# The first layer's projections on x times the norm weights, with the reciprocal root applied behind the products

## The chip, the cores and the metric

The kernel runs on one NeuronCore of a Trainium2 chip. The metric is device time in microseconds of one execution on that core, the lowest being best. Engines are named as the profile names them: PE multiplies matrices, DVE works on vectors, ACT computes activations and copies, POOL is the general engine, SP issues most of the DMAs. Each engine works through its own list of instructions.

## The reference, cut to what matters

A two-layer encoder over 256 tokens of width 1024. Each layer starts with a root mean square norm and one wide projection, whose output is cut into eleven parts.

```python
def rms_norm(x, g):
    y = xf * lax.rsqrt(jnp.mean(xf * xf, axis=-1, keepdims=True) + EPS)
    return (y * g).astype(x.dtype)

u = rms_norm(h, g_mix_pre)
(gq, gk, gv, gg, ra_f, ra_b, aq, ak, av, gate_a, gate_b) = jnp.split(u @ w_in, offsets, axis=-1)
```

`ra` gives the decay of a gated linear attention branch with `gq`, `gk`, `gv` and the output gate `gg`; `aq`, `ak`, `av` feed a grouped attention branch, in which q and k are normed once more per head and turned by rotary tables; the two gates mix the branches. Then follow an output projection, a gated feed-forward part and a per-layer embedding, each with its own norms. All data are float32; the products must have about that accuracy.

## The kernel before

**Products.** A product in float32 accuracy is made of three passes over operands split in a high part (fp32r) and a low remainder: high x high, high x low, low x high. Weights come from HBM in units of about 1 MB into two `raw` buffers. ACT casts a unit to its high part `wh` in two pieces, DVE subtracts to get the low part `wl` (`split`, line 130), and a `raw` buffer is loaded again when DVE has read it. Four `wh`/`wl` pairs exist, so casts run ahead of PE by a few units. The class `Stream` (line 245) gives out loads and splits in the order of the plan. Activations are kept transposed and split the same way in `uT`, a tile for each four of the eight 128-column blocks k of the 1024 columns, with the two token halves (hf) side by side.

**Stages.** In layer 0 the order is: the start (x, its norm, the first weights), the `rq` stage with the ranks and the attention's q (four weight units of 256 rows by 1056 columns, six accumulators: two token halves by the three column pieces of `RQ`), `kv`, `gqk`, `v`, `gg`, the gates, and so on. Layer 1 has the same stages with its norm made in another place.

**What sets the order.** The instruction order within an engine is partly written out: `on` (line 139) puts each instruction behind the one that the same engine got from `on` before it. All else is placed by a scheduler, which works from the order of the program, priorities and the dependences. Small tasks that have to wait for something are generators: each `tick` of a projection step lets them come nearer to their next part (`yield n` means after n ticks). `start` (line 792) is such a task.

**The start before.** x of the first token half is loaded in two parts by two queues, then the first weight unit in two pieces with x of the second half between them. Per half, ACT squares the first 512 columns (`square`), DVE the rest (`square_here`), POOL makes the reciprocal root (`rstd`), DVE multiplies x by it (`normed`, line 758), PE transposes the result, and ACT and DVE make high and low parts with the norm weight as a per-partition factor (`turned`, line 773), since behind the transpose the columns lie on partitions. The norm weights come as eight rows and are transposed by PE (`gains`, line 763). Before that PE multiplies constants (`warm_up`). `rq_first` (line 967) orders the first unit's products so that they start with what is there first.

**Behind the products.** `put_q` (line 945) squares the attention's q per head on ACT (`head_ss`), POOL makes the roots (`inv_sqrt`, line 447 and behind), DVE turns q with the rotary tables (`rope`). `put_ranks` (line 918) splits the 32 rank columns on DVE. `keys` (line 1003) does the same for k and splits v of the attention. The q and k of the linear branch are made transposed, with columns on partitions and tokens along the row, and are copied out of PSUM by ACT. The linear branch's v is split, its gate copied, and the mixing gates go through a sigmoid on ACT.

Of the kernel before, what the change touches and what calls it, by code (L numbers as in the profile page):

```python
# [10 lines left out]
F32 = mybir.dt.float32  # L11
# [39 lines left out]
WARM = 7, 3, 1  # L51
# [7 lines left out]
def trunk_kernel(ctx: ExitStack, tc: tile.TileContext, a: dict, out: bass.AP):  # L59
# [83 lines left out]

    keep = cp.tile([P, 512], BF16, tag="keep", name="keep")
# [5 lines left out]
    def load_x(hf, queues=(("dma", nc.sync), ("dma", nc.sync))):  # L150
        for j, (e, q) in enumerate(queues):
            c = slice(j * 512, (j + 1) * 512)
            on(e, q.dma_start, h[:, hf, c], a["x"][0, hf * P : (hf + 1) * P, c])

    load_x(0, (("dma", nc.sync), ("act", nc.scalar)))
# [612 lines left out]

    def split_here(hi, lo, src):
        on("act", nc.scalar.copy, hi, src)  # L770
        on("dve", nc.vector.tensor_tensor, out=lo, in0=src, in1=hi.bitcast(F32), op=ALU.subtract)

    def turned(hf, k, n):

        ps = aux()
        for i in range(n):
            on("pe", nc.tensor.transpose, ps[:, i * P : (i + 1) * P], xn[hf][:, (k + i) * P : (k + i + 1) * P], ident)
        hi, lo = uT.at(k, n, hf * P, P)
        if n == 4:
            y = t512()  # L780
# [11 lines left out]
    def start():  # L792
# [34 lines left out]
        for hf in range(2):  # L827
            normed(hf, 4, 4)
# [754 lines left out]
```

## Time and profile before

| what | value |
|---|---|
| device time, median of 3 runs | 924.73 us (923.97 to 925.41) |
| span of the profiled execution | 922.9 us |
| median of the runs less that span | 1.8 us |
| PE busy | 912.2 us, 99% of the span |
| DVE busy | 786.1 us, 85% |
| ACT busy | 578.5 us, 63% |
| POOL busy | 83.8 us, 9% |
| mean DMA rate | 188 GB/s |
| mean granted TensorE clock | 0.998 |

The profile is of one execution of its own, so its span is set beside the timed runs and not equal to them. A row of the order of time gives the start in us, the time from there to the end, the engine, the line of the kernel, the operation, what it writes and reads, and how many were put together; in brackets stands how long the engine was idle just before and what ended that. A name that ends in q (SPq, ACTq) is a queue that issues DMAs. A line 142 is the helper `on`, and the rows there are told apart by their tiles: `h` is x, `big_start` a tile of `uT`, `raw`, `wh` and `wl` the weights. Matmuls overlap, so their pace is read from one row's start to the next.

### The profile page before, as it was taken

To read this page: it belongs to the slowest core of one execution; us is meant where nothing else is said; L and a number is where in the kernel's file an instruction comes from. 1 tells how busy PE (TensorE), PEld (TensorE's weight loads), DVE (VectorE), ACT (ScalarE), POOL (GpSimd) and SP (SyncE) were. 2 spreads that over 40 slices of the span, in tenths; PEclk is the share of its full clock that TensorE was granted. 3 is DMA by queue.
4 is the path that set the end of the run, shared out by engine and by line. 5 is a ranking of instruction groups with operands and counts; after the bars stand their busy time and mean duration, and the time that the engine had idled before them with its cause. 6 is when DMAs were issued, how large, how long until landed. Compare 5 with 4: busy or idle time off the path is not lost.

```text
span 922.9 us, 12406 instructions
## 1 busy us (share of the span) xinstructions
PE 912.2 (99%) x4668; PEld 776.2 (84%) x4668; DVE 786.1 (85%) x1002; ACT 578.5 (63%) x954; POOL 83.8 (9%) x147
## 2 busy tenths in 40 slices
PE   9999999999999999999999999999999999999996
PEld 6898888888888888888899988888888888888885
DVE  6898989987579998999779789798875799989884
ACT  4669676664567656566676677765644766565563
POOL 3400211300000000000114001100001000000000
PEclk9999999999999999999999999999999999999999
DMA  7463455656286565647576424454573756545361
GB/s 260 144 230 134 148 173 188 201 193 232 90 277 222 178 233 168 265 128 268 188 256 220 153 92 137 137 191 174 195 260 104 268 177 204 223 177 217 126 239 45
DMA packets 88679, 173.44 MB, mean 188 GB/s; under 512 B 3422, under 2 KB 26470, under 8 KB 88108
## 3 DMA queue, kind: packets, MB, share of 16 engines
q1 hardware_dynamic: 88460, 172.40, 54.0%
q8 instruction: 36, 0.59, 0.3%
q10 hardware_dynamic: 160, 0.27, 0.1%
q14 instruction: 23, 0.19, 0.1%
HBM read 169.50 MB, written 3.15 MB: 187 GB/s over the span
## 4 chain that ended last, share of the span: by engine, by line
PE 94%; DVE 2%; ACT 1%; DMA 1%; issue 1%; POOL 0%; POOLq 0%; DVEq 0%; ACTq 0%; SPq 0%
PE acc_0ffnin L120 12%; PE acc_1ffnin L120 11%; PE acc_1gate L120 7%; PE acc_0gate L120 7%; PE acc_0ffnin L104 7%; PE acc_1ffnin L104 7%; PE acc_1rq L120 3%; PE acc_0gqk L120 2%; PE acc_0wout L120 2%; PE acc_1gqk L120 2%; PE acc_1ple L120 2%; PE acc_0ple L120 2%; PE acc_0gg L120 2%; PE acc_1gg L120 2%; PE acc_0v L120 2%; PE acc_1merge L120 2%
## 5 line engine op out<-in xcount | busy, mean ns | idle before, releaser
L104 PE MATMUL acc_0ffnin<-wh_0ffnin,big_0ffnin 128*128 128x512 f32 x176 | 56.9, 393 | 0.0
L104 PE MATMUL acc_1ffnin<-wh_1ffnin,big_1ffnin 128*128 128x512 f32 x176 | 56.8, 392 | 0.0
L132 ACT CAST wh_1ffnin<-raw_1ffnin 128x1024 fp32r<-128x1024 f32 x38 | 38.5, 1049 | 27.3 <-DMA raw_1ffnin<-in_w_ffn_out_dram 8.7
L132 ACT CAST wh_0ffnin<-raw_0ffnin 128x1024 fp32r<-128x1024 f32 x38 | 38.4, 1048 | 23.8 <-PE acc_0ffnin L120 7.8
L128 DVE TENSOR_TENSOR wl_1ffnin<-raw_1ffnin,wh_1ffnin 128x1024 fp32r<-128x1024 f32 x38 | 45.0, 1221 | 8.9 <-ACT wh_1ffnin L132 8.9
L128 DVE TENSOR_TENSOR wl_0ffnin<-raw_0ffnin,wh_0ffnin 128x1024 fp32r<-128x1024 f32 x38 | 44.8, 1220 | 7.1 <-ACT wh_0ffnin L132 7.0
L120 PE MATMUL acc_1ffnin<-wh_1ffnin,big_1wout 128*128 128x512 f32 x168 | 42.5, 393 | 0.0
L120 PE MATMUL acc_0ffnin<-wh_0ffnin,big_0wout 128*128 128x512 f32 x168 | 42.5, 393 | 0.0
L104 PEld LDWEIGHTS acc_0ffnin<-wh_0ffnin,big_0ffnin 128*128 128x128 f32 x176 | 33.0, 188 | 7.1 <-DVE big_0ffnin L128 0.5
L104 PEld LDWEIGHTS acc_1ffnin<-wh_1ffnin,big_1ffnin 128*128 128x128 f32 x176 | 33.1, 188 | 6.7
L128 DVE TENSOR_TENSOR wl_1ffnin<-lent_1ffnin,wh_1ffnin 128x1024 fp32r<-128x1024 f32 x30 | 35.8, 1218 | 1.7 <-ACT wh_1ffnin L132 1.7
L128 DVE TENSOR_TENSOR wl_0ffnin<-lent_0ffnin,wh_0ffnin 128x1024 fp32r<-128x1024 f32 x30 | 35.8, 1216 | 1.7 <-ACT wh_0ffnin L132 1.7
L120 PEld LDWEIGHTS acc_1ffnin<-wh_1ffnin,big_1wout 128*128 128x128 f32 x168 | 31.1, 188 | 6.2
L120 PEld LDWEIGHTS acc_0ffnin<-wh_0ffnin,big_0wout 128*128 128x128 f32 x168 | 31.1, 188 | 6.2
L132 ACT CAST wh_1ffnin<-lent_1ffnin 128x1024 fp32r<-128x1024 f32 x30 | 30.7, 1053 | 7.1 <-PE acc_1ffnin L104 3.9
L132 ACT CAST wh_0ffnin<-lent_0ffnin 128x1024 fp32r<-128x1024 f32 x30 | 30.7, 1054 | 6.7 <-PE acc_0ffnin L104 3.9
L104 PE MATMUL acc_0ffnin<-wl_0ffnin,big_0ffnin 128*128 128x512 f32 x88 | 34.3, 389 | 0.0
L104 PE MATMUL acc_1ffnin<-wl_1ffnin,big_1ffnin 128*128 128x512 f32 x88 | 34.3, 389 | 0.0
L128 DVE TENSOR_TENSOR wl_1gate<-raw_1gate,wh_1gate 128x1024 fp32r<-128x1024 f32 x20 | 23.6, 1219 | 5.4 <-ACT wh_1gate L132 5.3
L128 DVE TENSOR_TENSOR wl_0gate<-raw_0gate,wh_0gate 128x1024 fp32r<-128x1024 f32 x20 | 23.7, 1226 | 4.8 <-ACT wh_0gate L132 4.8
L132 ACT CAST wh_0gate<-raw_0gate 128x1024 fp32r<-128x1024 f32 x20 | 20.0, 1048 | 11.7 <-DMA raw_0gate<-in_w_o_attn_dram 5.6
L132 ACT CAST wh_1gate<-raw_1gate 128x1024 fp32r<-128x1024 f32 x20 | 20.0, 1049 | 11.5 <-DMA raw_1gate<-in_w_o_attn_dram 5.5
(695 smaller groups left out, 2691.8 us busy)
## 6 DMA issues: line engine op xcount, KB each, us to landing
raw_0ffnin<-in_w_ffn_out_dram SPq DMA_DIRECT2D x11, 1024.0 KB, 6.6
raw_1ffnin<-in_w_ffn_out_dram SPq DMA_DIRECT2D x11, 1024.0 KB, 5.1
lent_0ffnin<-in_w_ffn_in_dram SPq DMA_DIRECT2D x6, 1024.0 KB, 7.4
lent_1ffnin<-in_w_ffn_in_dram SPq DMA_DIRECT2D x6, 1024.0 KB, 8.3
raw_0v<-in_w_in_dram SPq DMA_DIRECT2D x4, 1024.0 KB, 4.9
raw_0gate<-in_w_o_gla_dram SPq DMA_DIRECT2D x4, 1024.0 KB, 4.9
raw_0gate<-in_w_o_attn_dram SPq DMA_DIRECT2D x4, 1024.0 KB, 5.1
raw_0wout<-in_w_ffn_in_dram SPq DMA_DIRECT2D x8, 512.0 KB, 4.9
```

The lines of the kernel that those rows point to most:

```text
L104: return nc.tensor.matmul(o, lhsT, rhs, start=start, stop=stop)
L120: nc.tensor.matmul(o, x, y, start=start and n == 0, stop=stop and n == len(seq) - 1, **kw)
L128: nc.vector.tensor_tensor(out=out, in0=in0, in1=in1, op=ALU.subtract)
L132: nc.scalar.copy(hi, src)
```

## The change

The first layer's projections read x times the norm weights. The reciprocal root, one number for each token, is left out of the products and applied behind them, at every place where a result leaves PSUM:

- q and k of the attention: the squares are taken of the product times the root (a `scale` of the activation), and the root of the head norm is multiplied by the token's root on POOL, one operation more (`inv_sqrt` with `by`).
- ranks, v of the attention, v of the linear branch: the cast and the subtraction take the root as a per-partition factor (`split_by` and in `put_ranks`).
- the gate `gg` and the two sigmoids: a `scale` of the activation.
- q and k of the linear branch have tokens along the row. For them the 256 roots are spread over all partitions: two diagonal matrices on DVE, two matmuls with ones on PE, a copy on ACT into `spread`; the copies out of PSUM become multiplications by it on DVE.

The start is laid anew. PE transposes x itself (`turn`), ACT makes the high part (`high`), DVE the low part (`rest`), block by block; squares and roots follow after the second unit's splits, and the rotary tables' loads and products move behind them. The loads go in the order x columns 0 to 511 of the first half, first weight unit in two pieces, second unit, x columns 512 to 1023 of both halves, all by SP; the norm weights and then x columns 0 to 511 of the second half by ACT. ACT casts the first weight piece in three parts. The products of the first unit go block by block over both halves. The warm-up is six matmuls of 128 columns on a constant from POOL, six of 512, and two of 128 behind the first transposes.

```diff
-WARM = 7, 3, 1
+WARM = 6, 6, 2
...
+    seed = cp.tile([P, P], BF16, tag="seed", name="seed")
+    on("pool", nc.gpsimd.memset, seed, 1.0)
...
-    def load_x(hf, queues=(("dma", nc.sync), ("dma", nc.sync))):
-        for j, (e, q) in enumerate(queues):
-            c = slice(j * 512, (j + 1) * 512)
-            on(e, q.dma_start, h[:, hf, c], a["x"][0, hf * P : (hf + 1) * P, c])
-    load_x(0, (("dma", nc.sync), ("act", nc.scalar)))
+    def load_x(hf, j, e="dma", q=nc.sync):
+        c = slice(j * 512, (j + 1) * 512)
+        on(e, q.dma_start, h[:, hf, c], a["x"][0, hf * P : (hf + 1) * P, c])
+    load_x(0, 0)
+    on("act", nc.scalar.dma_start, grow, a["g_mix_pre"][0].rearrange("(k p) -> k p", p=P))
+    load_x(1, 0, "act", nc.scalar)
...
-    def inv_sqrt(t, n, mul, add):
+    def inv_sqrt(t, n, mul, add, by=None):
...
+        if by is not None:
+            with in_turn():
+                last_pow[0] = nc.gpsimd.tensor_scalar(out=t, in0=t, scalar1=by, scalar2=None, op0=ALU.mult)
+    def split_by(hi, lo, src, r):
+        if r is None:
+            return split(hi, lo, src)
+        nc.scalar.activation(hi, src, AF.Copy, bias=0.0, scale=r)
+        nc.vector.scalar_tensor_tensor(
+            out=lo, in0=src, scalar=r, in1=hi.bitcast(F32), op0=ALU.mult, op1=ALU.subtract
+        )
...
-    x1 = [lambda: load_x(1)]
-    on("act", nc.scalar.dma_start, grow, a["g_mix_pre"][0].rearrange("(k p) -> k p", p=P))
-    ws.load(lambda: x1 and x1.pop()())
...
+    ws.load()
+    load_x(0, 1)
+    load_x(1, 1)
...
-    def warm_up(n):
+    def warm_up(n, wide=False):
+        x = keep if wide else seed
         for _ in range(n):
-            on("pe", mm, warm, keep[:, 0:P], keep, True, True)
+            on("pe", mm, warm[:, 0 : x.shape[-1]], seed, x, True, True)
...
+    warm_up(WARM[1], True)
...
-    ss, rs, xn = [small(2, "ss") for _ in range(2)], [small(1, "rstd") for _ in range(2)], [mid(), mid()]
+    ss = [small(2, "ss") for _ in range(2)]
+    rs, spread, ropes_first = [small(1, "rs", 2) for _ in range(2)], [], []
...
-    def normed(hf, k, n):
-        c = slice(k * P, (k + n) * P)
-        on("dve", nc.vector.tensor_scalar, out=xn[hf][:, c], in0=h[:, hf, c], scalar1=rs[hf], scalar2=None, op0=ALU.mult)
...
+    def low(hi, lo, src):
+        on("dve", nc.vector.tensor_tensor, out=lo, in0=src, in1=hi.bitcast(F32), op=ALU.subtract)
...
-        on("dve", nc.vector.tensor_tensor, out=lo, in0=src, in1=hi.bitcast(F32), op=ALU.subtract)
-    def turned(hf, k, n):
...
+        low(hi, lo, src)
+    banks = {}
+    def turn(hf, *ks):
+        if (hf, ks[0] // 4) not in banks:
+            banks[hf, ks[0] // 4] = aux()
+        for k in ks:
+            ps = banks[hf, k // 4][:, k % 4 * P : (k % 4 + 1) * P]
+            on("pe", nc.tensor.transpose, ps, h[:, hf, k * P : (k + 1) * P], ident)
+    def high(hf, *ks):
+        for k in ks:
+            ps = banks[hf, k // 4][:, k % 4 * P : (k % 4 + 1) * P]
+            on("act", nc.scalar.activation, uT.at(k, 1, hf * P, P)[0][:, 0, :], ps, AF.Copy, bias=0.0, scale=gcol[:, k : k + 1])
+    def rest(hf, *ks):
+        for k in ks:
+            ps = banks[hf, k // 4][:, k % 4 * P : (k % 4 + 1) * P]
+            hi, lo = (t[:, 0, :] for t in uT.at(k, 1, hf * P, P))
+            on("dve", nc.vector.scalar_tensor_tensor, out=lo, in0=ps, scalar=gcol[:, k : k + 1],
+               in1=hi.bitcast(F32), op0=ALU.mult, op1=ALU.subtract)
...
...
-        square(0, 0)
-        square_here(0, 1)
...
-        warm_up(WARM[1])
-        rstd(0)
-        on("act", nc.scalar.copy, unit_a[0], unit_a[2])
-        normed(0, 0, 2)
-        low(*first)
-        turned(0, 0, 2)
+        turn(0, 0)
+        turn(1, 0)
+        turn(0, 1)
+        turn(1, 1)
+        turn(0, 2, 3)
...
-        square(1, 0)
-        square_here(1, 1)
-        rstd(1)
-        low(*rest)
-        normed(1, 0, 2)
-        split_here(*unit_b)
+        high(0, 0)
+        high(1, 0)
+        for c in RQ:
+            on("act", nc.scalar.copy, *(t[:, slice(*c)] for t in unit_a[::2]))
+        rest(0, 0)
+        rest(1, 0)
+        low(*cut(unit_a, slice(0, 288)))
+        high(0, 1)
+        high(1, 1)
+        low(*cut(unit_a, slice(288, 1056)))
+        on("act", nc.scalar.copy, unit_b[0], unit_b[2])
+        rest(0, 1)
+        rest(1, 1)
+        high(0, 2, 3)
+        low(*unit_b)
+        rest(0, 2, 3)
...
-        turned(1, 0, 2)
-        normed(0, 2, 2)
-        normed(1, 2, 2)
-        yield 3
+        turn(1, 2, 3)
+        high(1, 2, 3)
+        rest(1, 2, 3)
+        yield 4
...
-        turned(0, 2, 2)
...
-        turned(1, 2, 2)
...
         for hf in range(2):
-            normed(hf, 4, 4)
+            square(hf, 0)
...
+        turn(0, 4, 5, 6, 7)
+        for hf in range(2):
+            square_here(hf, 1)
+            rstd(hf)
+        ropes_first.extend(rope_tables(0))
+        high(0, 4, 5, 6, 7)
+        rest(0, 4, 5, 6, 7)
+        yield 1
+        turn(1, 4, 5, 6, 7)
+        high(1, 4, 5, 6, 7)
+        rest(1, 4, 5, 6, 7)
...
+        both = mid()
+        diag, ones = both[:, 0:T], both[:, T : T + P]
+        nc.gpsimd.memset(ones, 1.0)
         for hf in range(2):
-            turned(hf, 4, 4)
+            s = slice(hf * P, (hf + 1) * P)
+            nc.vector.tensor_scalar(out=diag[:, s], in0=ident, scalar1=rs[hf], scalar2=None, op0=ALU.mult)
+        yield 4
+        ps = aux()
+        for hf in range(2):
+            s = slice(hf * P, (hf + 1) * P)
+            mm(ps[:, s], ones, diag[:, s], True, True)
+        spread.append(both[:, 512 : 512 + T])
+        nc.scalar.copy(spread[0], ps[:, 0:T])
...
+        rows = [None, None] if l else rs
...
+            ropes = ropes_first
...
-                ropes = rope_tables(0)
-            wup = up_weights(0)
+                wup = up_weights(0)
...
-        def head_ss(src, n, junk, ss):
+        def head_ss(src, n, junk, ss, hf):
+            by = {} if rows[hf] is None else {"scale": rows[hf]}
...
-                nc.scalar.activation(junk[:, s], src[:, s], AF.Square, accum_out=ss[:, i : i + 1])
+                nc.scalar.activation(junk[:, s], src[:, s], AF.Square, accum_out=ss[:, i : i + 1], **by)
...
...
+                else:
+                    nc.vector.tensor_scalar(
+                        out=r[:, :, 0:16].bitcast(F32R), in0=src, scalar1=rows[hf], scalar2=None, op0=ALU.mult
+                    )
+                    nc.vector.scalar_tensor_tensor(
+                        out=r[:, :, 32:48].bitcast(F32R), in0=src, scalar=rows[hf], in1=r[:, :, 0:16],
+                        op0=ALU.mult, op1=ALU.subtract,
+                    )
...
-                head_ss(src, n, dst, ss[:, hd : hd + n])
-                inv_sqrt(ss[:, hd : hd + n], n, 1.0, P * EPS)
+                head_ss(src, n, dst, ss[:, hd : hd + n], hf)
+                inv_sqrt(ss[:, hd : hd + n], n, 1.0, P * EPS, rows[hf])
...
-        def rq_first(os_, hf):
...
+        def rq_first(os_):
+            for k in range(2):
+                for hf, ps in ((0, (0, 2)), (1, (0, 2)), (0, (1,)), (1, (1,))):
...
-                            mm(os_[b][:, : c1 - c0], x, y, k + p == 0, False)
-                tick()
+                            mm(os_[hf, b][:, : c1 - c0], x, y, k + p == 0, False)
+                    tick()
...
-            elif b == 2:
-                rq_first([o[hf, i] for i in range(3)], hf)
+            elif (hf, b) == (1, 2):
+                rq_first(o)
...
-                    head_ss(o[hf], 2, kr, ss)
-                    inv_sqrt(ss, 2, 1.0 / P, EPS)
+                    head_ss(o[hf], 2, kr, ss, hf)
+                    inv_sqrt(ss, 2, 1.0 / P, EPS, rows[hf])
...
-                    split(avh[:, s], avl[:, s], o[hf][:, 256:512])
+                    split_by(avh[:, s], avl[:, s], o[hf][:, 256:512], rows[hf])
...
-                if x == 0:
+                if l == 0:
+                    nc.vector.scalar_tensor_tensor(
+                        out=dst, in0=src, scalar=1.0 if x else P**-0.5,
+                        in1=spread[0].unsqueeze(1).broadcast_to([P, 2, T]), op0=ALU.mult, op1=ALU.mult,
+                    )
+                elif x == 0:
...
         for j in range(2):
             for hf, o in enumerate(project(uT)):
-                split(*(t[:, hf, j * 512 : (j + 1) * 512] for t in v), o)
+                split_by(*(t[:, hf, j * 512 : (j + 1) * 512] for t in v), o, rows[hf])
...
             for hf in range(2):
-                nc.scalar.copy(gg[:, hf, j * 512 : (j + 1) * 512], o[hf])
+                dst = gg[:, hf, j * 512 : (j + 1) * 512]
+                if rows[hf] is None:
+                    nc.scalar.copy(dst, o[hf])
+                else:
+                    nc.scalar.activation(dst, o[hf], AF.Copy, bias=0.0, scale=rows[hf])
...
-                nc.scalar.activation(sgate[br][:, hf, j * 512 : (j + 1) * 512], src, AF.Sigmoid)
+                by = {} if rows[hf] is None else {"scale": rows[hf]}
+                nc.scalar.activation(sgate[br][:, hf, j * 512 : (j + 1) * 512], src, AF.Sigmoid, **by)
```

More of the change, by code (lines that the diff above doesn't have):

```diff
@@ L792, in start @@
+    def rest(hf, *ks):
[4 more added lines that the diff above has]
+               in1=hi.bitcast(F32), op0=ALU.mult, op1=ALU.subtract)
     def start():
         cut = lambda piece, c: [t[:, c] for t in piece]
-        def low(hi, lo, src):
-            on("dve", nc.vector.tensor_tensor, out=lo, in0=src, in1=hi.bitcast(F32), op=ALU.subtract)
@@ L965, in rq_step @@
             tick()
-        def rq_first(os_, hf):
-            uT.need(hf)
-            orders = (((0, 0, 2),), ((0, 1), (1, 0)), ((1, 2, 1),)), (((0, 0, 2),), ((1, 0, 2),), ((0, 1), (1, 1)))
-            for step in orders[hf]:
-                for k, *ps in step:
+        def rq_first(os_):
+            for k in range(2):
+                for hf, ps in ((0, (0, 2)), (1, (0, 2)), (0, (1,)), (1, (1,))):
                     ah, al = uT.tok(k, hf)
```

22 lines of the change are left out of this document (3 added, 19 removed).

## The prediction

> **What bounds the kernel now.** I read the page's busy times and chain first, then the waits of PE, then the order of time of each engine over the first 60 us, and the listing of the built programs' order, engine by engine, which shows what stands behind what.
>
> ```profile
> span 922.9 us, 12406 instructions
> PE 912.2 (99%) x4668; PEld 776.2 (84%) x4668; DVE 786.1 (85%) x1002; ACT 578.5 (63%) x954; POOL 83.8 (9%) x147
> PE 94%; DVE 2%; ACT 1%; DMA 1%; issue 1%; POOL 0%; POOLq 0%; DVEq 0%; ACTq 0%; SPq 0%
> ```
> ```profile
> PE warm L104 <- DVE keep L142: 1.6, 1, 1.6
> PE acc_0rq L120 <- ACT big_start L142: 0.6, 1, 0.6
> ...
> ```
>
> PE is busy all the time, and every wait of it worth naming lies in the first 25 us. So time is won or lost only where PE gets to its matmuls sooner or later, and behind the head nothing can take up a shift: a microsecond that PE loses there stays lost. The change is to be followed on PE from its first product to the point where all weights come ahead of it again.
>
> ```profile
> 1.65 3.17 PE L104 MATMUL warm<-keep 128*128 128x512 bf16 x7 [1.65 <-DVE keep L142]
> 4.95 1.46 PE L104 MATMUL warm<-keep 128*128 128x512 bf16 x3
> 6.78 0.69 PE L142 MATMUL aux_start<-ident,mid_start 128*128 128x128 f32 x2 [0.36 <-DVE mid_start L142]
> 7.26 0.63 PE L104 MATMUL warm<-keep 128*128 128x512 bf16 x1
> 7.92 2.13 PE L104 MATMUL acc_0rq<-wh_start,big_start 128*128 128x288 f32 x6
> 10.57 0.66 PE L104 MATMUL acc_0rq<-wl_start,big_start 128*128 128x384 f32 x2
> 11.06 0.51 PE L104 MATMUL acc_0rq<-wh_start,big_start 128*128 128x384 f32 x2
> 21.38 1.03 PE L142 MATMUL aux_start<-ident,mid_start 128*128 128x128 f32 x8
> 22.17 0.95 PE L120 MATMUL acc_0rq<-wh_start,big_start 128*128 128x384 f32 x4
> 24.09 1.40 PE L120 MATMUL acc_0rq<-wh_start,big_start 128*128 128x288 f32 x6 [0.63 <-ACT big_start L142]
> 30.25 0.69 PE L120 MATMUL acc_0rq<-wh_start,big_start 128*128 128x288 f32 x4
> 36.05 0.38 PE L934 MATMUL aux_0rq<-ident,t_0rq 128*81 128x128 f32 x2
> 36.18 2.07 PE L120 MATMUL acc_0kv<-wh_start,big_start 128*128 128x512 f32 x8
> 41.95 2.43 PE L120 MATMUL acc_0kv<-wh_0rq,big_start 128*128 128x512 f32 x10
> 44.22 0.62 PE L120 MATMUL acc_0kv<-wl_0rq,big_start 128*128 128x512 f32 x2
> 47.40 1.11 PE L120 MATMUL acc_0gqk<-big_start,wh_0rq 128*128 128x256 f32 x8
> ```
>
> Read from starts to starts: the first product stands at 7.92. The first projection has four weight units of 36 matmuls (12 of 288 and 24 of 384 columns); the fourth runs from 30.25 to 36.05, so a unit costs 5.8 us at full speed, and PE is through with the third (U from here on) at 30.25. The kv stage begins at 36.18, the gqk stage at 47.40; a 512 column matmul is (44.22 - 41.95)/10 = 0.227 us. A transpose takes (22.17 - 21.38)/8 = 0.1 us here and 0.24 at 6.78, where PE is slow: warm matmuls come every 0.43 us, and 384 columns get quick between 10.57 and 11.06. I put full speed at 10.7.
>
> ```profile
> 0.78 0.41 ACTq L142 DMA_DIRECT2D h<-in_x_dram  x1
> 1.23 0.58 ACTq L142 DMA_DIRECT2D mid_start<-in_g_mix_pre_dram  x1
> 5.73 1.07 ACT L142 CAST wh_start<-raw_start 128x1056 fp32r<-128x1056 f32 x1 [0.68 <-DMA raw_start<-in_w_in_dram]
> 7.50 0.62 ACT L142 ACTIVATE big_start<-aux_start,gcol_start 128x128 fp32r<-128x128 f32 x2 [0.70 <-PE aux_start L142]
> 25.93 3.95 ACT L132 CAST wh_start<-raw_start 128x1056 fp32r<-128x1056 f32 x4
> 33.04 0.28 ACT L916 ACTIVATE mid_0rq<-acc_0rq 128x128 f32<-128x128 f32 x1
> 33.29 0.28 ACT L916 ACTIVATE mid_0rq<-acc_0rq 128x128 f32<-128x128 f32 x1
> 48.16 0.37 ACT L132 CAST big_0kv<-acc_0kv 128x256 fp32r<-128x256 f32 x1
> ```
> ```profile
> 16.14 0.61 DVE L142 SCALAR_TENSOR_TENSOR big_start<-aux_start,gcol_start,big_start 128x128 fp32r<-128x128 f32 x2 [1.20 <-ACT big_start L142]
> 17.10 1.26 DVE L142 TENSOR_TENSOR wl_start<-raw_start,wh_start 128x1056 fp32r<-128x1056 f32 x1 [0.35 <-ACT wh_start L142]
> 32.01 0.19 DVE L928 CAST t_0rq<-acc_0rq 128x32 fp32r<-128x32 f32 x1 [2.34 <-PE acc_0rq L120]
> 32.43 2.35 DVE L128 TENSOR_TENSOR wl_start<-raw_start,wh_start 128x1024 fp32r<-128x1024 f32 x2
> 34.70 0.42 DVE L125 TENSOR_TENSOR mid_0rq<-acc_0rq,rope_0rq 128x256 f32<-128x256 f32 x1
> 43.74 3.49 DVE L128 TENSOR_TENSOR wl_0rq<-raw_start,wh_0rq 128x1024 fp32r<-128x1024 f32 x3
> ```
> ```profile
> h<-in_x_dram ACTq DMA_DIRECT2D x1, 256.0 KB, 3.7
> raw_start<-in_w_in_dram SPq DMA_DIRECT2D x3, 1056.0 KB, 5.0
> raw_start<-in_w_in_dram SPq DMA_DIRECT2D x2, 1024.0 KB, 4.9
> ```
>
> The reader is to see two things here. ACT casts the fourth unit and the first kv unit from 25.93 to 29.88, 4 us ahead of PE. And DVE stood idle 2.34 us up to 32.01 although the kv cast was done at 29.88: its queue had the rank copy, which waits for PE, ahead of the kv split. An engine does not step past a waiting instruction.
>
> **The change, part by part.** *Head.* Squares, root and normalizing leave the path to the first product; in their place stands x's second half. ACT's queue now issues the gains first (0.58) and that load at 1.4; by the 3.7 row it lands at 5.1. PE's order has the transposes of both halves mixed, and the first `high` waits for all six: 5.1 + 5 x 0.24 + 0.2 of drain = 6.5. Warm-up is over by then and costs nothing. Two `high` (0.62) make 7.1, the cast of 288 columns, about 0.4 between the 256 column row and the 1056 column row, 7.5. The first product gains 0.4 us and no more; the first weight piece, landed at 5.73, is ready.
>
> *First three units.* PE was slow for 3.4 us from 7.26 to 10.7; I take as much from 7.5, that is to 10.9, which does 1.7 us of work. Unit one with two transposes (5.8 + 0.2) ends at 10.9 + 4.3 = 15.2, four transposes 15.6, unit two with four more 21.8, unit three U = 27.6, against 30.25: 2.65 us won. Of these 0.4 are the head; the rest is what PE lost before between 7.92 and 30.25, 22.3 us for 20.1 of work, of which the 0.63 at 24.09 is the one wait that the profile names. Cover: DVE has 16 `rest` (0.305), two squares (1.4), and 7.7 us of splits before unit three's second half is there, 14 us from 6.8 on and some 1.3 of waits: 22.1, read by PE at 22.4. So that gap is closed, but barely. The third load is issued behind DVE's split of unit one at about 11.2, lands 5.0 later and is cast behind eight `high`, near 18.2 to 20.2. DVE loses six normalizing products, and four operations of 512 columns become eight `rest`. SP issues the gain of the later branch (128 KB) ahead of the third load while the load waits for DVE anyway, the six small loads between the third and fourth unit, and rope's four behind that; the fourth lands near 19 and rope's tables, on POOL by 27, are used after 33: nothing.
>
> *The spread.* The two matmuls that spread the roots stand on PE behind the whole third unit, and on ACT the copy of their result stands ahead of both casts of the fourth unit.
>
> ```profile
> 93.72 0.60 PE L104 MATMUL aux_0gla<-t_0gla,mid_0gla 128*128 128x128 f32 x4
> 94.16 0.39 PE L104 MATMUL aux_0gla<-mid_0gla 128*128 128x128 f32 x2
> ```
>
> That form costs 0.11, so 27.8; drain 0.17, copy 0.37, first cast 1.05: PE starts the fourth unit at 29.4 in place of 27.8, a stall of 1.6. The cover that the casts had at 25.93 is gone: their data is there from 19 on.
>
> *The fourth unit and kv.* It ends at 35.2, its transposes at 35.4. On ACT the casts of the first kv unit now stand behind all squares of the first half and six of the second, three of which need the last product: 35.2 + 0.17 + 3 x 0.25 + 1.05 = 37.2. PE waits 1.8 us, where before it waited for nothing. DVE then has the second half of the kv split as its 21st instruction behind the ranks: the first rope product can start after four squares, at 29.4 + 3.2 + 1.0 = 33.6. The 18 rope operations took 43.74 - 34.70 less one split (1.17) and 0.35 of ranks, 7.5 us; 17 of them (7.1), ranks 0.3 and two splits 2.34 put it at 43.4. PE, 20 matmuls and a pair of transposes after 37.2, is there at 41.95: a stall of 1.45. The other 28 matmuls end at 49.75, against 47.40.
>
> *Behind that.* The freed buffer delays the gqk load to 43.4 + 4.9 = 48.3, its casts to 49.35 and 50.35, where PE needs them at 49.75 and 50.35: just in time. The split behind it waits for POOL's three operations (one more than before) and comes 0.3 before PE. Four copies of q and k go from ACT to DVE, about 0.6 each, 2.4 us in all; DVE, 85% busy, has that much room before the next stage, so I take 0, with 0 and 0.8 as ends. The added multiplications on POOL end before the softmax asks for them. Scales in the v, gg and gate evictions change no count: 0. Sum: +2.35 us.
>
> The profiled span is 922.9, the median of the runs 924.73, so 1.8 us lie around the span; I add the change to the median: 924.73 + 2.35 = 927.1. A change under 0.2%, 1.85 us, is about what cannot be told from none.
>
> **Unknowns, with both ends.** x's second half can land from 4.7 (beside the first half's pace) to 5.7 (behind the weight piece): -0.4 to +0.6. The point of full speed is the largest: at best from the first product, which with quicker transposes makes U earlier by 1.8 (then DVE's splits hold PE), at worst a stretch later. [...]
>
> **The rivals.** [...] *Early clock*: the warm-up starts near 1.1 in place of 1.65 and opens the clock: U falls by 1.8, all that follows with it, 925.3, no change to tell. Against: six of its matmuls are narrower, the whole shorter than the warm-up that failed. *Faster*: the two waits in ACT's queue do not hold the casts behind them, as if ACT handed them out by their data. Then the stalls of 1.6, 1.8 and 1.45 go and the head's gain stands: 924.73 - 2.5 = 922.2. It decides once less than 0.6 us of these 4.85 is left. Against it: the idle DVE at 32.01. [...]
>
> **How the numbers follow.** Forecast 0.60, of which 0.14 within 0.2% (the landing earlier, stalls a few tenths shorter); late clock 0.14; early clock 0.10; faster 0.16. So faster 0.16, same 0.24, slower 0.60. The forecast's own range is 926.2 to 928.2; taking in both clock cases gives 925.0 to 929.0, and leaves out the faster case and little above.
>
> **What will show it.** First product near 7.5; U near 27.6; then PE waiting on ACT for the fourth unit's weights (1.6) and for kv's (1.8), and on DVE for kv's low part (1.45); gqk starting near 49.8. In ACT's waits, the copy of the spread and the squares are released by PE. The prediction is wrong if PE's waits name none of these, if U is below 26, or if the shift at gqk does not stay to the end.

## The result, and the profile after

The changed kernel takes 933.1 us (median of four runs, 932.0 to 935.5) against 924.9 us before: a ratio of 1.0092, 95% interval 1.0077 to 1.0107. It is slower, by 8 us, where 2.4 were forecast and 929.0 was the upper end of the range. The profiled execution, which was the fastest of the four, has a span of 930.0 us, 7.1 more than before.

The first lines of the page, and the waits of PE in the changed kernel (us in total, times, longest):

```profile
span 930.0 us, 12441 instructions
PE 913.3 (98%) x4675; PEld 778.5 (84%) x4675; DVE 785.5 (84%) x1006; ACT 580.8 (62%) x959; POOL 86.6 (9%) x157
```
```profile
PE acc_0kv L120 <- ACT wh_start L132: 2.9, 1, 2.9
PE acc_0rq L120 <- ACT wh_start L132: 1.4, 1, 1.4
PE aux_start L142 <- DMA h<-in_x_dram: 1.1, 1, 1.1
...
PE acc_0kv L120 <- DVE wl_start L128: 0.8, 1, 0.8
PE acc_0gqk L120 <- ACT wh_0rq L132: 0.5, 1, 0.5
```

PE does hardly more work than before (913.3 us busy against 912.2); it waits. The waits that the prediction named are there (fourth unit 1.4, kv 2.9 and 0.8), beside two that it did not name: x's second half at the head, and the gqk weights. PE's order of time has the places:

```profile
6.15 0.77 PE L142 MATMUL aux_start<-ident,h 128*128 128x128 f32 x5 [1.12 <-DMA h<-in_x_dram]
6.76 0.28 PE L104 MATMUL warm<-seed 128*128 128x128 bf16 x2
7.95 3.65 PE L104 MATMUL acc_0rq<-wh_start,big_start 128*128 128x288 f32 x12 [0.92 <-ACT wh_start L142]
28.26 0.61 PE L104 MATMUL aux_start<-mid_start 128*128 128x128 f32 x4
30.30 1.62 PE L120 MATMUL acc_0rq<-wh_start,big_start 128*128 128x288 f32 x9 [1.43 <-ACT wh_start L132]
36.20 0.38 PE L988 MATMUL aux_0rq<-ident,t_0rq 128*81 128x128 f32 x2
39.49 4.51 PE L120 MATMUL acc_0kv<-wh_start,big_start 128*128 128x512 f32 x12 [2.91 <-ACT wh_start L132]
43.84 0.63 PE L120 MATMUL acc_0kv<-wl_start,big_start 128*128 128x512 f32 x2
46.90 1.20 PE L120 MATMUL acc_0kv<-wl_start,big_start 128*128 128x512 f32 x4 [0.83 <-DVE wl_start L128]
54.02 1.69 PE L120 MATMUL acc_0gqk<-big_start,wh_0rq 128*128 128x256 f32 x9 [0.49 <-ACT wh_0rq L132]
```

The third unit ends at 28.26 (U), 2.0 us earlier than before. The spread takes that back at once: 0.6 us of products and a wait of 1.43, and the fourth unit starts at 30.30, where it started at 30.25 before. From there the kernel only loses: kv starts 3.3 us later than before, gqk (54.02) 6.6, v 7.2. Behind v nothing is gained or lost worth naming, since the whole span is 7.1 longer. The places of v, before and after (the two times are the first and the last start of a group):

```profile
L120 PE MATMUL acc_0v<-wh_0gqk,big_start x48: 389/389/476, 76.0 to 96.7; 128*128 128x512 f32 x48
```
```profile
L120 PE MATMUL acc_0v<-wh_0gqk,big_start x48: 389/389/476, 83.2 to 103.8; 128*128 128x512 f32 x48
```

Two rows need a second look. The 12 products from 39.49 to 43.84 take 0.36 us each, not 0.227. The table by stretches (width, PE busy, granted clock, DMA share, GB/s) shows why:

```profile
9.00:10.00 1.00, 1.00 (x5) 0.50 1.02 402
38.00:39.00 1.00, 0.00 (x0) 1.00 0.00 0
39.00:39.50 0.50, 0.01 (x1) 0.80 0.00 0
40.00:42.00 2.00, 2.00 (x6) 0.50 0.01 4
42.50:43.00 0.50, 0.50 (x3) 0.79 0.00 0
```

PE's granted clock fell to one half at the end of the 2.9 us gap, at 39.3, and stayed there for 3.4 us. The head has such a stretch too, from 8.6 to 12.0. PE had been quick before it: the five transposes from 6.15 to 6.76 came every 0.12 us. But between 4.95 and 7.95 it mostly stood still, for x's second half and then for the first weights. The other row is 46.90, where PE waits for DVE. The rows of ACT, DVE, POOL and SP's queue, in this order:

```profile
28.90 0.37 ACT L880 COPY mid_start<-aux_start 128x256 f32<-128x256 f32 x1 [7.26 <-PE aux_start L104]
33.51 0.37 ACT L961 ACTIVATE mid_0rq<-acc_0rq,rs_start 128x128 f32<-128x128 f32 x1 [2.29 <-PE acc_0rq L120]
33.87 0.36 ACT L961 ACTIVATE mid_0rq<-acc_0rq,rs_start 128x128 f32<-128x128 f32 x1
...
38.32 2.06 ACT L132 CAST wh_start<-raw_start 128x1024 fp32r<-128x1024 f32 x2
52.92 2.00 ACT L132 CAST wh_0rq<-raw_start 128x1024 fp32r<-128x1024 f32 x2 [1.26 <-DMA raw_start<-in_w_in_dram]
```
```profile
35.12 0.42 DVE L125 TENSOR_TENSOR mid_0rq<-acc_0rq,rope_start 128x256 f32<-128x256 f32 x1 [1.22 <-ACT mid_0rq L961]
40.29 0.25 DVE L977 TENSOR_SCALAR t_0rq<-acc_0rq,rs_start 128x32 fp32r<-128x32 f32 x1 [1.76 <-POOL t_0rq L968]
45.63 1.21 DVE L128 TENSOR_TENSOR wl_start<-raw_start,wh_start 128x1024 fp32r<-128x1024 f32 x1
```
```profile
39.75 0.31 POOL L461 TENSOR_SCALAR qss_0rq<-qss_0rq,rs_start 128x3 f32<-128x3 f32 x1
40.00 0.26 POOL L968 MEMSET t_0rq<- 128x192 f32 x1
```
```profile
32.74 14.55 SPq L297 DMA_DIRECT2D raw_start<-in_w_in_dram  x2
```

The squares come 0.34 us apart (0.25 before). ACT, with 14 of them in its queue, gets to the kv casts at 38.32. DVE stands 1.76 us for a memset of the second half's rank tile, which lies in POOL's queue behind nine root operations (three more than before; the row of 39.75 is the last of them). So the second half of kv's low part is done at 46.8; the gqk load, second of SP's two issues, goes out only then and lands at 52.92. Two chains therefore run side by side from 30 to 54: PE with its gap and its half clock, and DVE with its ropes and its wait. They meet at 46.9 within 0.8 us.

### The profile page after: what moved, and what is told of

It is laid out like the page before. It is cut to its first block, busy times and chain, and to the rows that moved or that the text cites. A ratio compares the mean times of both kernels' runs of the same rounds, so it can differ in the third digit from the quotient of the medians.

```text
span 930.0 us, 12441 instructions
## 1 busy us (share of the span) xinstructions
PE 913.3 (98%) x4675; PEld 778.5 (84%) x4675; DVE 785.5 (84%) x1006; ACT 580.8 (62%) x959; POOL 86.6 (9%) x157
## 4 chain that ended last, share of the span: by engine, by line
PE 90%; DVE 3%; DMA 2%; ACT 2%; issue 1%; POOL 1%; ACTq 0%; POOLq 0%; DVEq 0%; SPq 0%
PE acc_1ffnin L120 11%; PE acc_0ffnin L120 11%; PE acc_0gate L120 7%; PE acc_1gate L120 7%; PE acc_1ffnin L104 6%; PE acc_0ffnin L104 6%; PE acc_1rq L120 2%; PE acc_0gqk L120 2%; PE acc_0wout L120 2%; PE acc_1gqk L120 2%; PE acc_1ple L120 2%; PE acc_0ple L120 2%; PE acc_0gg L120 2%; PE acc_1gg L120 2%; PE acc_0v L120 2%; PE acc_0merge L120 2%
```

## The experiments

One measure serves for all: the distance from U to the starts of kv, gqk and v in the profiled execution, which does not depend on the head. Each variant is an edit of the changed kernel. (Before, and in h_all4, where the spread stands later, U is the start of the fourth unit. In f_casts and the two h kernels the scheduler put the first gqk products ahead of kv's last ones, so their gqk column stands too early to be compared; v can be.) Times are medians; 924.7 to 925.3 was measured for the kernel before beside them.

| kernel | U | kv − U | gqk − U | v − U | time us |
|---|---|---|---|---|---|
| before | 30.3 | 5.9 | 17.2 | 45.7 | 924.9 |
| changed | 28.3 | 11.2 | 25.8 | 54.9 | 933.1 |
| PE kept busy (e_warm) | 31.6 | 11.3 | 25.2 | 55.0 | 934.3 |
| casts ahead of squares (f_casts) | 29.0 | 8.1 | 18.4 | 49.7 | 928.7 |
| copy on DVE (c_dve) | 29.8 | 10.1 | 24.3 | 53.3 | 933.1 |
| rank tiles early (d_sets) | 29.9 | 11.9 | 25.7 | 54.7 | 933.2 |
| no root in squares (b_noptr) | 28.2 | 9.1 | 27.5 | 56.6 | 934.4 (one run) |
| x's half first (g_xfirst) | 25.8 | 11.2 | 26.1 | 55.2 | 930.2 |
| g + PE kept busy (i_warm) | 25.5 | 11.2 | 25.1 | 54.2 | 929.8 |
| g + rank tiles early (i_sets) | 25.4 | 11.9 | 24.9 | 54.1 | 930.3 |
| g + both (i_both) | 25.2 | 11.9 | 23.3 | 52.6 | 928.0 |
| g + copy on DVE (j_dve) | 25.8 | 10.1 | 24.8 | 53.9 | 928.6 |
| f, d, g and a late spread (h_all4) | 25.8 | 6.0 | 16.7 | 46.2 | 921.5 |
| f, d, g, copy on DVE (h_all3) | 27.2 | 7.0 | 16.4 | 46.8 | 923.7 |

**Is the half clock the loss?**

```
 (put_ranks, behind the two transposes of the first half)
+            for _ in range(24 if l + hf == 0 else 0):
+                mm(ps[:, 256:512], seed, keep[:, 0:256], True, True)
```

> The changed kernel with 24 idle products (bf16, 256 columns) on PE behind the fourth unit's rank transposes, so that PE has no gap in front of the first kv unit; what is computed stays the same. Both theories expect the first kv product still at 39.5, because ACT's casts set it, and the first 12 kv products at 0.227 us each in place of 0.36, with a granted clock of 1.0 in place of 0.5. Theory 'queue' (the end is set by DVE, whose second half of the first kv unit's low part is done at 46.8 and whose buffer the gqk load waits for): PE only waits longer for that low part, 2.4 us in place of 0.8, gqk still starts at 54.0 and the time does not move (within 0.5 us of the changed kernel, 933). Rival 'clock' (the 3.4 us of half clock are themselves 1.6 us of the loss): gqk starts near 52.4 and the time falls by 1.6 us, to 931.5.

934.3 us (932.2 to 936.5, five runs), ratio 1.0097, interval 1.0081 to 1.0113. PE's order of time:

```profile
39.75 2.78 PE L104 MATMUL aux_0rq<-keep,seed 128*128 128x256 bf16 x24
42.83 3.02 PE L120 MATMUL acc_0kv<-wh_start,big_start 128*128 128x512 f32 x12 [0.30 <-ACT wh_start L132]
46.71 0.73 PE L120 MATMUL acc_0kv<-wl_start,big_start 128*128 128x512 f32 x2 [0.86 <-DVE wl_start L128]
50.24 1.19 PE L120 MATMUL acc_0kv<-wl_start,big_start 128*128 128x512 f32 x4 [1.19 <-DVE wl_start L128]
```

The 12 products now take 3.0 us in place of 4.5 (the mean granted clock of the run is 0.998, against 0.995), and PE stands for DVE instead (0.86 and 1.19 us). The time does not fall: the half clock lay under DVE's chain. In this execution U itself is 3.3 us late, which belongs to the head (below).

**Does the order on ACT carry it?** The squares of layer 0 are ordered behind the second kv cast.

```
+        kv_cast.append(last_cast[0])          (start, behind ws.fill())
-                nc.scalar.activation(junk[:, s], src[:, s], AF.Square, accum_out=ss[:, i : i + 1], **by)
+                with tc.issue_after(kv_cast[0].ins) if l == 0 else nullcontext():
+                    nc.scalar.activation(junk[:, s], src[:, s], AF.Square, accum_out=ss[:, i : i + 1], **by)
```

> The changed kernel with the squares of the first projection queued on ACT behind both casts of the first kv unit. Theory 'queue': the casts run from 31.2 to 33.3, kv starts at 36.6 behind the fourth unit without a wait, DVE has both low parts by 36.3 and the gqk load is issued then, not at 46.9; what is left is one wait for the second low part of the second kv unit (DVE near 46.4, PE there at 44.3), so gqk starts near 49.6, 4.4 us earlier than in the changed kernel, and the time is near 928.7. Rival 'loads and clock' (the loss is from late loads and a slow start of PE whatever the order on ACT): gqk stays above 52.5 and the time above 931.5.

928.7 us (928.5 to 930.0, five runs), ratio 1.0040, interval 1.0026 to 1.0054.

```profile
37.07 2.07 PE L120 MATMUL acc_0kv<-wh_start,big_start 128*128 128x512 f32 x8
```

kv follows the fourth unit without a wait, the time is the one expected for this run, and more than half of the loss is gone with one edge on ACT. The first gqk products came earlier than expected (18.4 us behind U in place of some 21), because 13 of them stand ahead of kv's last four. Before v, PE waited 1.1 us for the scaled keys, and DVE for POOL's roots to scale them by:

```profile
55.94 0.68 DVE L1072 TENSOR_SCALAR t_0kv<-t_0kv,kss_0kv 128x128 f32<-128x128 f32 x3 [1.27 <-POOL kss_0kv L463]
```

**The copy of the spread, and POOL's memsets.**

```
-        nc.scalar.copy(spread[0], ps[:, 0:T])
+        nc.vector.tensor_copy(spread[0], ps[:, 0:T])
```

> The changed kernel with the copy of the spread roots moved from ACT to DVE, so that nothing on ACT stands between the third unit and the casts of the fourth. Theory 'queue': the fourth unit's casts run near 21.6 to 23.7, PE starts the fourth unit at 28.9 in place of 30.3, and since squares, kv casts and DVE's ropes all hang on PE's products of that unit, everything behind shifts by the same 1.4 us: kv at 38.1, gqk at 52.6, time 931.7. Rival 'covered' (the 1.4 us are taken up by what stands next, as the kv load or POOL's roots): kv or gqk stay where they are, and the time at 933.

```
-            r = t512()[:, 0:192].rearrange("p (d r) -> p d r", d=2)      (put_ranks, with its three memsets)
+            r = empty[hf] if l == 0 else rank_tile()                      (both tiles made and set ahead of the steps)
```

> The changed kernel with the three POOL memsets of the second half's rank tile issued at the head, beside the first half's, and no longer behind POOL's nine root operations. Theory 'queue': DVE loses the 1.76 us wait at 40.3; kv still starts at 39.5 with the clock at half; the second low part is done at 45.0 in place of 46.8, PE does not wait for it, the gqk load is issued 1.8 us earlier, and gqk starts near 52.7; with its casts no longer late the time falls by 1.8 us, to 931.3. Rival 'POOL is not what holds DVE' (the wait is only named after POOL, and ACT's slower squares hold the ropes as well): DVE waits as long elsewhere, gqk stays at 54, time 933.

Neither moved the time: 933.1 (ratio 1.0087, interval 1.0073 to 1.0100) and 933.2 (1.0086, 1.0072 to 1.0099). The traces suggest why, and the reasons differ. With the copy on DVE the distance to v fell by 1.6 us, near the 1.4 expected, but x's second half landed at 6.9 in its profiled run and U was 1.5 late. With the rank tiles early DVE's wait for POOL is gone, yet the scheduler put all 16 squares ahead of the casts, PE's gap became 3.6 us and its clock stayed at one half until 47:

```profile
41.00:47.00 6.00, 5.15 (x12) 0.50 0.00 1
```

**Is it the price of the root as an operand?** The squares are taken without `scale`.

```
-            by = {} if rows[hf] is None else {"scale": rows[hf]}      (head_ss)
+            by = {}
```

> The changed kernel with the sums of squares of the first layer's heads taken without the root (no scale operand; it leaves out the factor inside the square, so q and k norms of layer 0 come out unscaled). The casts of the first kv unit come out behind 11 and 14 squares in place of 14 and 14. Theory 'pointer' (a root read as a scale operand makes each square 0.09 us longer): squares come every 0.25 us in place of 0.34, the first cast ends 4.8 us after the first square's start less than 4.0, kv starts 9.1 us behind the end of the third unit's products in place of 11.2, and the wait in front of kv is 0.8 in place of 2.9, short enough that the clock stays up. Rival (squares are paced by reading PSUM or by reading out the sum): they stay 0.34 apart and kv moves by one us, the three squares fewer, alone.

```profile
33.40 0.28 ACT L961 ACTIVATE mid_0rq<-acc_0rq 128x128 f32<-128x128 f32 x1 [2.24 <-PE acc_0rq L120]
33.67 0.27 ACT L961 ACTIVATE mid_0rq<-acc_0rq 128x128 f32<-128x128 f32 x1
```
```profile
37.34 3.01 PE L120 MATMUL acc_0kv<-wh_start,big_start 128*128 128x512 f32 x12 [0.81 <-ACT wh_start L132]
42.90 1.20 PE L120 MATMUL acc_0kv<-wl_start,big_start 128*128 128x512 f32 x4 [1.08 <-DVE wl_start L128]
46.43 2.07 PE L120 MATMUL acc_0kv<-wl_start,big_start 128*128 128x512 f32 x4 [2.33 <-DVE wl_start L128]
```

The pace is 0.25 again, so the operand is the 0.09 us, and the wait ahead of kv is 0.8 as expected. But the time of its one run, 934.4, is no better: PE now reaches DVE's low parts early, waits 3.4 us there, and the granted clock falls to 0.50 in that gap instead, at 45.7, with products every 0.43 us from 48.30 to 51.72. What was true of the engine was not true of the time.

**The head.** The traces so far have x's second half landing at 6.15, 6.2, 6.2, 6.9, 7.4 and 7.9, all with the issue at 1.40, and the wait of PE for it reaching from 1.1 to 2.9 us. In the changed kernel's trace the issue stands beside those of the first three weight pieces on SP's queue:

```profile
1.40 0.37 ACTq L142 DMA_DIRECT2D h<-in_x_dram  x1
```
```profile
1.24 1.37 SPq L142 DMA_DIRECT2D raw_start<-in_w_in_dram  x3
```

```
-    on("act", nc.scalar.dma_start, grow, a["g_mix_pre"][0].rearrange("(k p) -> k p", p=P))
     load_x(1, 0, "act", nc.scalar)
+    on("act", nc.scalar.dma_start, grow, a["g_mix_pre"][0].rearrange("(k p) -> k p", p=P))
```

> The changed kernel with two transfers of ACT's queue exchanged: the first columns of x's second half first (issued at 0.78 in place of 1.40), the gains of the norm behind it. In five profiled runs of the changed kernel and its variants that half landed 6.15, 6.2, 6.9, 7.4 and 7.9 us after the start, the third unit ended between 28.3 and 31.6, and the four times of the changed kernel lie 3.5 us apart. Theory 'landing' (the late and uncertain landing beside the weight pieces is why the head gains nothing): it lands near 4.7, the first product stands near 7.0, the third unit ends near 27.4, the times lie within 1 us of one another and their median falls by 2, to 931. Rival 'the clock or the weights hold the head': the first product stays at 8 or above and the time at 933.

930.2 us (929.6 to 930.9, five runs), ratio 1.0054, interval 1.0041 to 1.0068.

```profile
4.74 1.18 PE L142 MATMUL aux_start<-ident,h 128*128 128x128 f32 x6
6.95 2.40 PE L104 MATMUL acc_0rq<-wh_start,big_start 128*128 128x288 f32 x12 [0.92 <-ACT wh_start L142]
```

All six transposes run without a wait from 4.74, the first product stands at 6.95, and the 12 products of 288 columns are through in 2.2 us where the changed kernel took 3.5 (7.95 to 11.41): PE keeps its pace in this head, where the granted clock was one half from 8.6 to 12.0 in the changed kernel. So of the 2.5 us in U, 1.0 is the first product and 1.2 the pace of these 12. U is 25.8, better than expected (27.4), the median falls by 2.9 us, and the runs lie within 1.4 us in place of 3.5. The landing was the head's limit, and its scatter fits a median of the changed kernel one microsecond above its profiled run. An early landing does not make the pace sure: six of the seven profiled runs with it have U at 25.2 to 25.8, but in h_all3 the first 12 products took 3.4 us and U is 27.2. That the weight pieces are what delays it is argued from the order of issue; the run shows that the place in the queue decides.

**The two chains, with the head settled.** The idle products and the early rank tiles again, each alone and together, on top of g_xfirst.

> x's second half first on ACT's queue (as g_xfirst, which took 930.2), and 24 idle products on PE in front of kv. The base: from the end of the third unit's products to kv 11.2 us, to gqk 26.1, to v 55.2. Theory 'two chains' (PE with its wait and its half clock, and DVE with its wait for POOL and 17 rope products ahead of the kv low part, reach the same place within a us of one another, so that mending one alone moves nothing): the clock stays up, PE waits for DVE instead, gqk at 25 to 26, v at 55.0, time 930.0. Rival 'one chain' (one of the two is the limit, and mending it gives its whole size): 1.6 us less here if it is the clock, v at 53.6, time 928.6.

> x's second half first on ACT's queue, and both rank tiles set at the head, so that DVE does not wait for POOL. All 16 squares come out ahead of the kv casts in place of 14, so kv starts 11.9 us behind the third unit's products. Theory 'two chains': DVE's second low part is there 16.7 us behind the third unit in place of 18.6, but PE, longer idle and at half clock for some 6 us, does not need it before; gqk at 25.8, v at 54.7, time 929.8. Rival 'one chain': 1.8 us less if it is DVE, v at 53.4, time 928.4.

> Both at once, with 30 idle products, since the gap is now 3.6 us. Theory 'two chains': now that neither holds, kv runs its 48 products at full clock from 11.9 without a wait, its end is at 23.2, the gqk load, issued at 16.8, lands at 22.8 and its first cast is done at 23.9, where gqk starts; v at 53.1, 2 us earlier than the base, time 928.2. Rival 'one chain': no more than the better of the two alone.

929.8, 930.3 and 928.0 us, with ratios of 1.0060 (1.0048 to 1.0072), 1.0061 (1.0049 to 1.0074) and 1.0035 (1.0022 to 1.0047), against 1.0054 for the base. So in the times either alone is nothing and both together are 2.2 us. The distances to v, 54.2, 54.1 and 52.6 against 55.2, say it less sharply: each alone came out 0.8 and 0.6 below what the two chains gave, about halfway to the rival. One profile cannot decide that, because the slow stretch is not of one length. Behind the same gap of 2.9 us the next 12 products took 4.4 us in the changed kernel (granted clock 0.50 for 3.4 us) and in c_dve, but 5.3 in g_xfirst and j_dve; behind 3.6 us the next ten took 4.4 in d_sets (0.50 for 6.8 us) and 3.6 in i_sets. By the granted 0.50, 3.4 us more cost up to 1.7, so a base with the long stretch flatters both variants. The medians carry the reading: the cover is large, and whether it is total is not shown. With both, PE has no wait left in kv but 0.3 in front, and 14 products take 3.5 us (the mean granted clock of the run is 0.998):

```profile
37.14 3.51 PE L120 MATMUL acc_0kv<-wh_start,big_start 128*128 128x512 f32 x14 [0.34 <-ACT wh_start L132]
```

**The copy on DVE once more, with the head settled.**

> x's second half first on ACT's queue (as g_xfirst, 930.2), and the copy of the spread on DVE. With the copy moved alone the distance from the third unit's products to v was 53.2 us against 54.9 in the changed kernel, yet the time stayed at 933, with the landing at 6.9 in its profiled run. Theory 'landing hid it' (the copy's 1.5 us are real, and were covered up by a late landing in the runs before): with the landing made early, v stands 53.5 behind the third unit and the time is 928.6, 1.6 below g_xfirst. Rival 'covered': 930.2 again, with the gain given back behind v.

928.6 us (928.4 to 928.6, five runs), ratio 1.0039, interval 1.0025 to 1.0052: 1.6 below g_xfirst (1.5 when each is set against the runs of the kernel before beside it), with v 53.9 behind U. The stall of the spread was worth its size. That a late landing hid it in c_dve's other runs as well fits, but only the profiled one shows it.

**All repairs.** Casts ahead, rank tiles early, x's half first, and the spread moved behind the first kv products (below); beside it the same with the spread left in place and its copy on DVE.

```
 (start)
-        yield 4
+        yield 16
         ps = aux()
```

> The changed kernel with the squares behind the first kv casts, both rank tiles set at the head, the spread of the roots moved behind the first kv products, and x's second half first on ACT's queue. Theory 'queue and landing': PE goes from the third unit (end near 27.4) straight into the fourth and into kv (near 33.6) at full clock, gqk starts near 45.5 in place of 47.4 in the kernel before and 54.0 in the changed one; DVE, with four evictions of q and k more, then holds PE some 2 us in the gqk stage, as it did with the casts alone (31.3 us from there to v, where the kernel before took 28.6). Time between 922.7 and 925.5, so level with the kernel before or a little faster. Rival (something not named yet costs the rest): above 927.

> As the last, but the spread stays behind the third unit and only its copy moves, from ACT to DVE. Theory 'queue': the two spread products cost PE 0.6 us and DVE's copy stands ahead of the fourth unit's low parts, which PE then waits for, 0.3 to 0.6 us; the rest as in the last, so about 1 us slower than it, 924 to 926.5. Rival (the place of the spread does not matter once the casts are ahead): the same time as the last.

The first takes 921.5 us (920.8 to 924.8, nine runs): a ratio of 0.9970 to the kernel before, interval 0.9959 to 0.9980. That is below what both theories expected. The second takes 923.7 (0.9988, 0.9979 to 0.9997), 2.2 us more, of which the trace shows 1.4 in U (27.2 against 25.8, with its first 12 products in 3.4 us against 2.2) and 0.6 behind it, among that 0.3 in which PE waits for the fourth unit's low part behind DVE's copy. The two kernels have the same head, so the 1.4 is not shown to come from the spread's place, which is worth between 0.6 and 2.2. The last three of PE's waits in h_all4, and its places:

```profile
PE acc_0rq L104 <- ACT wh_start L144: 0.9, 1, 0.9
PE aux_start L144 <- DMA mid_start<-in_g_mix_pre_dram: 0.4, 1, 0.4
PE aux_1at L104 <- DVE mid_1at L128: 0.2, 1, 0.2
```
```profile
25.76 0.87 PE L120 MATMUL acc_0rq<-wh_start,big_start 128*128 128x288 f32 x5
31.59 0.38 PE L998 MATMUL aux_0rq<-ident,t_0rq 128*81 128x128 f32 x2
31.72 0.95 PE L120 MATMUL acc_0kv<-wh_start,big_start 128*128 128x512 f32 x3
```

The list names no wait of PE between the first product and layer 1. From U to v it takes 46.2 us, 0.5 more than before, which is about the spread's own products. DVE's four evictions more, feared at 2 us in its expectation, cost nothing there. What is left of the gain is the head: 4.5 us in U, 4.0 at v, 3.4 in the medians.

## Why the prediction was wrong, step by step

The direction and the mechanism were right: products behind casts, casts behind squares, on a queue that does not step past a waiting instruction (waits of 1.43 and 2.91 us). f_casts and h_all4 show it, with kv 8.1 and 6.0 us behind U in place of 11.2, and the rival that ACT hands out its work by data is refuted. The sizes were wrong: the landing of x's second half, the wait ahead of kv and the time of DVE's low part all came out larger than summed. Two terms were missing: PE's clock behind a gap (0.50 for 3.4 us from 39.3), and the memset in POOL's queue (1.76 us).

**Head.** The landing was put at 5.1, from the 3.7 us row of a load that was issued first on its queue; its bound upward was 5.7. It landed at 6.15 at best and 7.9 at worst, with its issue among those of the weight pieces. The first product stood at 7.95, not 7.5, and gained nothing. g_xfirst prices the landing, with what it does to the clock, at 2.9 us in the median, more than the whole sum.

**First three units.** U = 27.6 was forecast, 28.26 measured; 0.45 is the first product. The sum let PE be slow for 3.4 us from the first product on, until 10.9; the granted clock was at one half for 3.4 us, until 12.0. That the size fits is luck. The sum took a PE that was not quick yet, while in this execution it was quick by 6.15 (transposes every 0.12 us) and its granted clock fell at 8.6. So the rival "early clock" had its condition, and lost it: g_xfirst, where PE does not stand still for x, keeps its pace (the first 12 products in 2.2 us) and has the U of that rival, 25.8. That the standing still is what slowed it is argued from these two traces and from b_noptr, with transposes every 0.12 us and then 12 products in 3.6 us; in the other four profiles of this head PE was still slow when x came, with transposes every 0.22 us. The late clock, and with it the upper end of the range, 929.0, let PE stay slow for 6.8 us from the first product on, 3.4 more than the sum; that was the author's estimate, and no run shows it: in the changed kernel the granted clock was back at 1.00 at 12.0, 4.1 us behind the first product, and in f_casts, where that stands at 8.57, transposes came every 0.07 us from 12.72 on.

**The spread.** 1.6 forecast; 1.43 of wait. This step was right (j_dve: 1.6 in time).

**The fourth unit and kv.** 1.8 of wait was forecast, 2.9 came. The sum let three squares stand behind the last product, at 0.25. They were not held by PE but by their own pace: with the root as an operand 14 squares took 4.8 us from 33.51, and ACT was through 2.1 us after PE. Of the 2.3 us by which kv started later than forecast, 0.9 is the later start of the fourth unit. In b_noptr, without the operand, the squares come every 0.25 us in place of 0.34. The prediction took the squares at the 0.25 of the kernel before and had no term for the added operand. It also missed what the gap does to the clock, 12 products at 0.36. DVE's low part was put at 43.4 and came at 46.8: the ropes began 1.5 later than forecast (0.9 with the fourth unit, the rest behind the slower squares), and the 1.76 for POOL's memset was missing. The POOL queue had been followed for the roots, not for what stands behind them.

**Behind that.** "Just in time" for the gqk load at 43.4 turned, with 3.4 us of delay on DVE, into a late load: 0.49 of wait, and then nine gqk products that take 1.53 us in place of 1.08, which is put down to the second cast, done at 54.92; that is 0.45 of the 0.6 lost between gqk and v. The copies on DVE show no cost of their own in these rows, as taken.

Added up to v: 2.35 forecast, 7.2 measured. The difference of 4.9 is 0.7 in U, 0.2 in the start of the fourth unit beside that, 1.4 up to kv, 2.0 from kv to gqk (half clock and DVE, one covering most of the other) and 0.6 behind gqk. The rest of the 8.2 in the medians, 1 us, fits the scatter of the landing and of the clock (U from 28.2 to 31.6 in the six profiles of this head); run by run it is not shown.

## What to carry to other kernels

When a change puts work on a queue, list all that lies behind the waiting instruction on that queue and then on the queues which wait for it, down to memsets and the load that a freed buffer lets go. When two chains end side by side, mending one can show nothing: test them together before calling either harmless. And look at the place of a transfer in time, not only its size: a small load issued 0.6 us later, among the big ones, came 1.5 to 3 us later.

## What the hardware showed that was not expected

- PE's granted clock fell to 0.50 at 8.6 and at 39.3 in the changed kernel, for 3.4 us each time, at 40.5 in d_sets, for 6.8 us, and at 45.7 in b_noptr. In the 3.4 us before each of these falls PE had worked for 0.7 to 1.5; a single gap of 1.4 us behind full work, at 28.9 in the changed kernel, left the clock at 1.00. The length did not follow the gap: behind 2.9 us of waiting the next 12 products took 4.4 us (changed kernel, c_dve) or 5.3 (g_xfirst, j_dve), and behind 3.6 us the next ten took 4.4 (d_sets) or 3.6 (i_sets). The granted clock does not show why PE is slow at first: in f_casts it stands at 1.00 while the first 12 products take 3.7 us.
- With idle products in the gap (e_warm) the row of the 12 products behind them is 3.0 us long in place of 4.5.
- A square with its sum and a per-partition scale came every 0.34 us, without the scale every 0.25, for 128 columns.
- 256 KB issued at 1.40 us beside two weight pieces of 528 KB and one of 1056 KB landed between 6.15 and 7.9 in six profiled runs of the same start; issued at 0.78 it was there by 4.7.
